# Weight loads between the adaLN loads of the first block, and a new order of loads and row ends in the last phase

## The chip, the cores and the metric

The kernel runs on one core of a Trainium2 chip. The metric is the device time of one execution, in microseconds; before the change the median of three runs is 3001.27 us. The engines are TensorE (PE, with its weight loads as PEld), VectorE (DVE), ScalarE (ACT), GpSimd (POOL) and SyncE (SP). In this kernel SP only issues DMAs, and it issues all of them, in one order that is fixed when the kernel is built.

## The reference

The input x has 2048 rows of 1024 channels. It is RMS-normalised, modulated by shift and scale that come from a condition vector (adaLN), and projected to all inputs of two branches: a gated causal convolution with a layer norm, and an RWKV-7 time mixing. Both are projected, gated, added, projected out and added to x; a final RMSNorm closes it.

```
mod = einsum('bd,de->be', silu(c), ada_w) + ada_b
shift, scale, gate = split(mod, 3)
h = rmsnorm(x, norm_g) * (1 + scale) + shift
p = h @ w_in
c_val, c_gate, c_og, ts, r_og, g_conv, g_rwkv = split(p)
y_conv = conv_branch(...)                      # ends in: silu(layernorm(u)) * silu(c_og) @ w_conv_out
y_rwkv = rwkv7_branch(...)                     # ends in: (layernorm(o) + bonus) * silu(r_og) @ w_rwkv_out
m = sigmoid(g_conv) * y_conv + sigmoid(g_rwkv) * y_rwkv
x = x + gate * (m @ w_out)
out = rmsnorm(x, final_g)
```

## The kernel before

The rows are worked in four blocks of 512 (TB), the channels in eight tiles of 128 (KT, k). Every large product is taken in single precision as three products of rounded halves: both operands are split into hi and lo, and hi by hi, lo by hi and hi by lo are summed in PSUM (mm3k, L207 to L215). A tile of 128 output columns is 24 matmuls of 512 columns, or in the first phase 48 of 256. Its weights are 512 KB; in block 0 load_w (L179) loads them as w_st (L189), ACT casts hi (L192), POOL or DVE subtracts for lo (L194), and both halves are stored to DRAM (L199, L200), from where later blocks load them ready made. The buffers for weights (tag w) are seven.

**First phase, block 0 (hprep0, L386).** Sixteen loads of 512 KB (L236) bring the adaLN rows for shift and scale, and DVE sums each of them against silu(c) (L237). From these come, per k, one column of shift and scale (ACT, L914 and L915). For each k PE transposes and normalises x (ps_x, L408), ACT applies shift and scale (hf, L411), ACT casts h_hi (L371) and DVE subtracts h_lo (L372). Four "front" tiles of the input projection run along with h: LORA, K, R and V (ps_f), whose weights are loaded at k = 0, 2, 4 and 5. The weights of R and V have buffers of their own (w_f). After them come the fifth tile, the low-rank products of the first pair of heads (aux<-lw,wl, L484), the pair's norms (ACT's sq, L519), its scores and solve (aux<-uv,As, L623, is the first product behind the scores), and so on through 70 further tiles.

**Last phase (L1014 on).** For each block the two branches' outputs are projected: rproj (eight tiles ps_main, times a gate into mr, L1023), then cproj (eight tiles, added to mr and split to m_hi, m_lo). The out-projection makes four column blocks (cb) of 256 columns, each of 96 matmuls in two accumulators pout (L1121 to L1123); addx (L1129) adds x to them on DVE, in two row tiles a buffer. finish (L1133 to L1144) ends a tile of 128 rows: a sum of squares, rsqrt in ten small DVE operations, two products with final_g (fg, L1142) and two stores. For the next block, osplit (L982 on) loads three operands for each of eight columns (ot, bt, rt, five buffers of tag ld), POOL adds and multiplies (L992, L993), ACT casts and DVE subtracts (L970, L971); lnorm (L1045 on) loads eight y (L1051), sums them on POOL (L1054), subtracts the mean (L1059), squares and sums (L1063), and makes u_hi, u_lo for the next cproj. Some names are reused by tiles of other stages, so that osplit's columns appear as m_lo<-ot,m_hi in the profile.

The order of the instructions on each engine is decided by a scheduler at build time that plays the program through with costs and priorities; "issue_after(ins)" adds that what stands under it follows ins on that engine. In block 0 the weight loads of the front had that condition on the last adaLN load issued so far, but the next adaLN load had none on them. In the last phase, osplit and lnorm of the next block were written ahead of the loads of x, and the finish of a block ahead of the next rproj.

## Time and profile before

| what | before |
|---|---|
| median of 3 runs (lowest, highest) | 3001.27 us (3000.13, 3005.64) |
| profiled execution | 3002.41 us |
| its span, granted clock of the core | 3000.7 us, 0.975 |
| busy: PE, DVE, ACT, POOL | 2817.7, 2049.1, 942.6, 1250.8 us |
| DMA: share of 16 engines' span in the hardware queue | 68.4% |

A row of a timeline gives start, duration, engine, line, operation, out<-in, the form, the count of merged instructions and, in brackets, the idle time before it with what ended it. A row of waits gives what the engine waited for, the total, how often, and the longest.

### The profile page before, as it was taken

The numbers are of one execution on the slowest core, as the hardware profiler recorded it, in microseconds if no ns is written. First come the engines' busy times: TensorE is split into PE (matmuls) and PEld (weight loads), VectorE is DVE, ScalarE is ACT, GpSimd is POOL, SyncE is SP. The second block draws the span as 40 slices with busy tenths as digits, with TensorE's granted clock in tenths as the row PEclk, the third lists the DMA queues.
The fourth block names the chain that finished last, engine by engine and source line by source line (L and its number), as shares of the span: only waits on it lengthen the run. The fifth ranks groups of instructions, "written<-read, shape, count | busy, mean of one in ns | idle before, by whom it ended". The sixth has DMA issues, their size and how long they took to land.

```text
span 3000.7 us, 64775 instructions
## 1 busy us (share of the span) xinstructions
PE 2817.7 (94%) x25672; PEld 2645.0 (88%) x25672; DVE 2049.1 (68%) x3871; ACT 942.6 (31%) x1779; POOL 1250.8 (42%) x1786
## 2 busy tenths in 40 slices
PE   6899998999999999899999989999999998899998
PEld 6889898989989989898999989999989988687988
DVE  6587878777767676867776767777689534768433
ACT  5433434332323242323231414132333212333201
POOL 3465555525343425243434355526367014555000
PEclk9999999999999999999999999999999999999999
DMA  8666758664768579747475777656547678879674
GB/s 314 210 239 215 252 202 289 229 219 153 265 194 282 163 252 299 233 152 228 144 245 164 253 241 249 206 184 194 181 160 279 219 266 305 319 285 347 241 282 168
DMA packets 367697, 699.24 MB, mean 233 GB/s; under 512 B 135265, under 2 KB 154017, under 8 KB 367394
## 3 DMA queue, kind: packets, MB, share of 16 engines
q1 hardware_dynamic: 367394, 695.10, 68.4%
q8 instruction: 202, 3.31, 0.4%
q14 instruction: 101, 0.83, 0.1%
HBM read 506.14 MB, written 187.70 MB: 231 GB/s over the span
## 4 chain that ended last, share of the span: by engine, by line
PE 44%; DMA 17%; DVE 14%; POOL 12%; issue 5%; SPq 4%; ACT 3%; POOLq 0%; DVEq 0%; ACTq 0%
PE ps_main L215 32%; POOL TT L653 4%; POOL itmp L651 4%; DMA La<-dA 2%; DMA w_st<-w_ro_t 2%; DMA w_st<-w_in_t 2%; DVE acc L800 2%; PE pout L1121 1%; PE pout L1122 1%; PE pout L1123 1%; PE aux L553 1%; DMA w_gr<-grow_d 1%; PE xo L715 1%; DMA w_st<-w_co_t 1%; SPq L637 1%
## 5 line engine op out<-in xcount | busy, mean ns | idle before, releaser
L215 PE MATMUL ps_main<-h_hi,w_hi 128*128 128x256 f32 x4608 | 947.4, 284 | 13.4 <-ACT w_hi L192 6.4
L215 PE MATMUL ps_main<-h_hi,w_lo 128*128 128x256 f32 x4608 | 948.5, 285 | 9.3 <-POOL w_lo L194 5.1
L215 PE MATMUL ps_main<-h_lo,w_hi 128*128 128x256 f32 x4608 | 954.6, 285 | 0.0
L215 PEld LDWEIGHTS ps_main<-h_hi,w_hi 128*128 128x128 f32 x4608 | 718.2, 191 | 24.8 <-ACT w_hi L192 7.1
L215 PEld LDWEIGHTS ps_main<-h_hi,w_lo 128*128 128x128 f32 x4608 | 717.2, 191 | 17.5 <-POOL w_lo L194 6.5
L215 PEld LDWEIGHTS ps_main<-h_lo,w_hi 128*128 128x128 f32 x4608 | 719.2, 191 | 8.6 <-issue 0.5
L800 DVE SCALAR_TENSOR_TENSOR acc<-u,ck,acc 128x512 f32<-128x512 f32 x928 | 697.9, 752 | 20.7
L651 POOL TENSOR_TENSOR itmp<-La,TT 128x126 f32<-128x126 f32 (+22 forms) x496 | 182.0, 367 | 162.6 <-DMA La<-dA 127.4
L653 POOL TENSOR_TENSOR TT<-TT,itmp 128x126 f32<-128x126 f32 (+22 forms) x496 | 188.0, 379 | 36.7
L707 ACT ACTIVATE Se<-S,pe 128x128 f32<-128x128 f32 x256 | 88.9, 394 | 243.9 <-DVE S L725 243.5
L194 POOL TENSOR_TENSOR w_lo<-w_st,w_hi 128x1024 fp32r<-128x1024 f32 x47 | 114.6, 2438 | 117.2 <-ACT w_hi L192 107.2
L725 DVE TENSOR_TENSOR S<-xo,Se 64x128 f32<-64x128 f32 x256 | 73.4, 287 | 99.4 <-PE xo L721 96.9
L192 ACT CAST w_hi<-w_st 128x1024 fp32r<-128x1024 f32 x71 | 74.4, 1048 | 193.8 <-DMA w_st<-w_in_t 159.1
L717 DVE TENSOR_TENSOR uv<-xo,rn 64x256 f32<-64x256 f32 x128 | 53.8, 420 | 95.1 <-PE xo L715 93.8
L712 DVE TENSOR_TENSOR XO<-xo,XO 128x256 f32<-128x256 f32 x128 | 53.7, 420 | 82.5 <-PE xo L710 65.2
L588 POOL TENSOR_TENSOR BK<-BK,pe 128x1024 f32<-128x1024 f32 x32 | 62.5, 1953 | 106.9 <-PE aux L553 86.4
L710 PE MATMUL xo<-S,KR 128*128 128x128 f32 x512 | 82.9, 284 | 19.6 <-DVE S L725 19.6
L563 DVE TENSOR_TENSOR As<-aux,maskA 128x512 f32<-128x512 f32 x128 | 82.8, 684 | 23.2 <-PE aux L553 22.1
L553 PE MATMUL aux<-KR,BK 64*128 64x128 f32 x1024 | 90.5, 293 | 8.3 <-POOL KR L541 5.1
L721 PE MATMUL xo<-uv,tk 128*128 128x128 f32 x512 | 81.8, 282 | 15.6 <-DVE uv L717 15.6
L715 PE MATMUL xo<-XO,As 64*64 64x64 f32 x1024 | 90.7, 227 | 5.5 <-DVE XO L712 5.4
L715 PEld LDWEIGHTS xo<-XO,As 64*64 64x64 f32 x1024 | 71.0, 136 | 25.7 <-DVE XO L712 6.7
(303 smaller groups left out, 5246.7 us busy)
## 6 DMA issues: line engine op xcount, KB each, us to landing
w_hi<-kh_in SPq DMA_DIRECT2D x219, 512.0 KB, 5.4
w_lo<-kl_in SPq DMA_DIRECT2D x219, 512.0 KB, 4.3
w_st<-w_in_t SPq DMA_DIRECT2D x73, 512.0 KB, 4.7
kh_in<-w_hi SPq DMA_DIRECT2D x71, 512.0 KB, 2.9
kl_in<-w_lo SPq DMA_DIRECT2D x71, 512.0 KB, 3.8
w_hi<-kh_ro SPq DMA_DIRECT2D x32, 512.0 KB, 6.3
w_lo<-kl_ro SPq DMA_DIRECT2D x32, 512.0 KB, 5.8
w_hi<-kh_co SPq DMA_DIRECT2D x32, 512.0 KB, 4.9
```

Of the source, the lines that this page charges most:

```text
L192: nc.scalar.copy(hi, st)
L194: lo_eng.tensor_tensor(out=lo, in0=st, in1=hi.bitcast(F32), op=ALU.subtract)
L215: nc.tensor.matmul(ps[:, qs], ww[:, k, :], aa[k][:, qs], start=(k == 0 and t == 0 and q == 0), stop=(k == KT - 1 and t == 2 and q == ms - ...
L553: return nc.tensor.matmul(pA[hh][:, c // 2, es], BK[hs, cc, es], KR[hs, cc, es], start=(c == 0), stop=(c == 3), skip_group_check=True)
L563: nc.vector.tensor_tensor(out=Asb[:, hh, c4 * 4:c4 * 4 + 4, :].rearrange("p (a e) n -> p a (e n)", e=2), in0=pA[hh], in1=flat(maskA).unsqu ...
L651: nc.gpsimd.tensor_tensor(out=tmp[:, :ni, :nt], in0=La[:, j:j + 1, j + 1:].broadcast_to([P, ni, nt]), in1=TT[:, :ni, j:j + 1].broadcast_to ...
L653: nc.gpsimd.tensor_tensor(out=TT[:, :ni, j + 1:], in0=TT[:, :ni, j + 1:], in1=tmp[:, :ni, :nt], op=ALU.add)
L707: nc.scalar.mul(Se[:, q, :], Sg[:, q, :], R[q]["pe"][:, c:c + 1])
L710: nc.tensor.matmul(xo[:, q, :], R[q]["KR"][:, cc, es], Sg[:, q, :], start=(q == 0), stop=(q == 1), skip_group_check=True)
L715: nc.tensor.matmul(xo[pr_, q, hs], As[q][pr_, hh, c, kcol(e)], XO[pr_, c, q, hs], start=(q == 0 and hh == 0), stop=(q == 1 and hh == 1), s ...
L721: last = nc.tensor.matmul(xo[:, 2 + q, :], R[q]["tk"][:, c, :], uv[:, c, q, :], start=False, stop=(q == 1), skip_group_check=True)
L800: nc.vector.scalar_tensor_tensor(out=acc if i + 1 < HALO else yj, in0=u[:, i:i + TB], scalar=ck[:, j, i:i + 1], in1=acc, op0=ALU.mult, op1 ...
```

## The change

It has three parts. In hprep0 each adaLN load behind the first follows the last weight load that was issued, so that the front's weights come between the adaLN loads; the stores and the small weights of the first pair follow the last adaLN load (front_ld). In the last phase, block 0 loads x first, and fg, osplit(1) and lnorm(1) issue their loads behind it. And finish of blocks 0 to 2 no longer stands ahead of the next rproj: two row tiles are finished behind its mr of n = 2, two behind n = 4.

```diff
     def load_w(name, n, hl=None, held=None):
...
-        nc.sync.dma_start(st, wsrc[name][n])
+        ada_ld[0] = nc.sync.dma_start(st, wsrc[name][n]).ins
...
         for k in range(KT):
-            next(ada_steps)
+            if k:
+                with tc.issue_after(ada_ld[0]):
+                    next(ada_steps)
+            else:
+                next(ada_steps)
...
+        front_ld.append(ada_ld[0])
         with tc.issue_after(ada_ld[0]):
             for store in held:
                 store()
...
-            with tc.issue_after(ada_ld[0]):
+            with tc.issue_after(front_ld[0]):
                 nc.sync.dma_start(wf, w2a2[pr])
...
-    def rproj(b, ohl, mr):
+    def rproj(b, ohl, mr, between=None):
...
-                nc.vector.scalar_tensor_tensor(out=mr[n], in0=th, scalar=1.0, in1=ppr, op0=ALU.add, op1=ALU.mult)
+                made = nc.vector.scalar_tensor_tensor(out=mr[n], in0=th, scalar=1.0, in1=ppr, op0=ALU.add, op1=ALU.mult)
+            if between and n in (2, 4):
+                with tc.issue_after(made.ins):
+                    for tt in (n - 2, n - 1):
+                        between(tt)
...
-    nc.sync.dma_start(fg, final_g.unsqueeze(0).broadcast_to([P, D]))
...
+    def xload(b):
...
+        return xts, ld.ins
+
+    for b in range(NB):
+        if b:
+            mhi, mlo = okt(b, MOFF)
+            cproj(b, uhl, (mhi, mlo))
+        if b == 0:
+            xts, ld = xload(0)
+            with tc.issue_after(ld):
+                nc.sync.dma_start(fg, final_g.unsqueeze(0).broadcast_to([P, D]))
+                ohl = osplit(1)
+                uhl = lnorm(1)
+        elif b + 1 < NB:
+            ohl = osplit(b + 1)
+            uhl = lnorm(b + 1)
+        if b:
+            xts, _ = xload(b)
...
         if b + 1 < NB:
-            for tt in range(NTT):
-                finish(tt)
-        if b + 1 < NB:
             mr = mnew()
-            rproj(b + 1, ohl, mr)
+            rproj(b + 1, ohl, mr, finish)
```

What it moves, at three places. SP's queue in the front, before: ada_st are the adaLN loads, w_st the weights (LORA, K, then R and V together, then the fifth tile), kh and kl the stores, ck and wf small operands.

```order
L236 DMA ada_st<-ada_t 128x1024 x5
L189 DMA w_st<-w_in_t 128x1024
L236 DMA ada_st<-ada_t 128x1024 x6
L199 DMA kh_in_830<-w_hi 128x1024
L200 DMA kl_in_831<-w_lo 128x1024
L434 DMA ck<-convk 128x248
L477 DMA wf<-w2a 128x256
L199 DMA kh_in_834<-w_hi 128x1024
L189 DMA w_st<-w_in_t 128x1024 x2
L200 DMA kl_in_835<-w_lo 128x1024
L189 DMA w_st<-w_in_t 128x1024
```

And with the change, from the same place on:

```order
L236 DMA ada_st<-ada_t 128x1024
L191 DMA w_st<-w_in_t 128x1024
L236 DMA ada_st<-ada_t 128x1024 x4
L191 DMA w_st<-w_in_t 128x1024
L236 DMA ada_st<-ada_t 128x1024 x2
L191 DMA w_st<-w_in_t 128x1024
L236 DMA ada_st<-ada_t 128x1024 x4
L201 DMA kh_in_830<-w_hi 128x1024
L202 DMA kl_in_831<-w_lo 128x1024
L201 DMA kh_in_834<-w_hi 128x1024
L202 DMA kl_in_835<-w_lo 128x1024
```

K's weights move four adaLN loads forward, those of R and V from behind the sixteenth to behind the tenth and the twelfth; the last four adaLN loads now follow V.

SP's queue in the out-projection of block 0, with the change (before, its order there is fg, then the eight y with the loads of osplit's fifth and sixth column between them, two ct, four xt, and only then the next w_lo and w_hi of the o projection; the loads of osplit's first four columns stand further ahead, among the weights of cproj). xt is x for rows 256 to 511; those for the first 256 rows stand earlier in both.

```order
L188 DMA w_lo<-kl_o_1_18069 128x1024
L187 DMA w_hi<-kh_o_0_19938 128x1024
L1108 DMA xt_31631<-x_in 128x512
L1108 DMA xt_31633<-x_in 128x512
L1108 DMA xt_31635<-x_in 128x512
L1108 DMA xt_31637<-x_in 128x512
L1120 DMA fg<-final_g 128x1024
L990 DMA ot<-o_d_0_75 128x512
L990 DMA bt<-bv_d_0_107 128x512
L990 DMA rt<-ro_d_0_139 128x512
L990 DMA ot<-o_d_1_76 128x512
L990 DMA bt<-bv_d_1_108 128x512
```

x stands ahead of y, and all columns of osplit(1), from the first on, stand behind x and fg; the eight y follow these rows, and behind the y the other weights of the o projection.

DVE at the start of rproj(1), before: rs is the rsqrt of the row ends, xt<-xt,rs,fg their products, and mr<-rth,ps_main what empties the accumulator of a tile of rproj (mr_32452 the first tile's).

```order
L133 SCALAR_TENSOR_TENSOR rs_t<-rs_t,vs 128x1 x2
L134 SCALAR_TENSOR_TENSOR rs_32379<-rs_t,rs_32379 128x1
L1136 TENSOR_REDUCE vs<-sq_31903 128x1
L134 SCALAR_TENSOR_TENSOR rs_32398<-rs_t,rs_32398 128x1
L1136 TENSOR_REDUCE vs<-sq_31903 128x1
L1142 SCALAR_TENSOR_TENSOR xt_31887<-xt_31887,rs_32379,fg 128x512
L1142 SCALAR_TENSOR_TENSOR xt_31889<-xt_31889,rs_32379,fg 128x512
L1142 SCALAR_TENSOR_TENSOR xt_31891<-xt_31891,rs_32398,fg 128x512
L1142 SCALAR_TENSOR_TENSOR xt_31893<-xt_31893,rs_32398,fg 128x512
L1137 TENSOR_SCALAR vs<-vs 128x1 x2
L971 TENSOR_TENSOR o_lo_33020<-ot,o_hi_33021 128x512
```

With the change (mr_32376 is the first tile's, mr_32378 the third's):

```order
L1084 TENSOR_SCALAR dg<-ident,rv 128x128 x4
L976 TENSOR_TENSOR m_lo_31654<-ot,m_hi_31646 128x512
L976 TENSOR_TENSOR m_lo_31655<-ot,m_hi_31647 128x512
L1028 SCALAR_TENSOR_TENSOR mr_32376<-rth,ps_main 128x512
L1028 SCALAR_TENSOR_TENSOR mr_32377<-rth,ps_main 128x512
L227 SCALAR_TENSOR_TENSOR y_31737<-th,y_31737 128x512
L1097 TENSOR_TENSOR y_31737<-y_31737,ct 128x512
L227 SCALAR_TENSOR_TENSOR y_31739<-th,y_31739 128x512
L227 SCALAR_TENSOR_TENSOR y_31742<-th,y_31742 128x512
L1097 TENSOR_TENSOR y_31739<-y_31739,ct 128x512
L976 TENSOR_TENSOR u_lo<-y_31737,u_hi 128x512
L1028 SCALAR_TENSOR_TENSOR mr_32378<-rth,ps_main 128x512
```

Before, the first mr stands three rows behind the last one quoted, after the ends of rows 0 and 1; now it follows osplit's last column, and the products of the first two row tiles stand between the fourth and the fifth mr.

11 lines of the change are left out of this document (2 added, 9 removed).

## The prediction

> **What bounds the kernel now.** I read the page first (busy times), then busy time in stretches to find where TensorE is not full, then PE's waits in those stretches, and last the timelines of the engines named there.
>
> ```profile
> PE 2817.7 (94%) x25672; PEld 2645.0 (88%) x25672; DVE 2049.1 (68%) x3871; ACT 942.6 (31%) x1779; POOL 1250.8 (42%) x1786
> ```
>
> PE is busy for 2817.7 of 3000.7 us, so a gain has to come out of the 183 us in which it stands still, or out of a clock below full. The change touches two places where that happens, the first 65 us and the stretch from 2500 to 2680. The columns are the stretch, its length, busy PE, PEld, DVE, ACT and POOL with counts, the granted clock, the DMA share and GB/s:
>
> ```profile
> 20.00:40.00 20.00, 18.06 (x127) 16.97 (x126) 20.00 (x31) 13.49 (x27) 2.74 (x2) 1.00 1.03 411
> 40.00:60.00 20.00, 14.56 (x96) 13.48 (x96) 7.52 (x13) 10.63 (x17) 8.61 (x5) 0.83 0.62 220
> 2500.00:2600.00 100.00, 81.90 (x528) 74.55 (x527) 65.28 (x138) 40.79 (x83) 56.37 (x43) 0.90 0.85 303
> 2600.00:2640.00 40.00, 35.85 (x149) 28.35 (x148) 16.75 (x22) 4.90 (x8) 22.16 (x15) 0.96 1.04 411
> 2640.00:2680.00 40.00, 39.89 (x206) 33.40 (x205) 25.68 (x43) 9.19 (x15) 16.62 (x12) 1.00 0.80 285
> ```
>
> At 20 to 40 us DVE has no gap and the DMAs are full; at 40 to 60 PE idles. From 2500 to 2600 PE idles 18 us, and from 2600 to 2640 the DMAs are full. What PE waits for in the first 125 us, and then from 2480 to the end (total, times, longest):
>
> ```profile
> PE aux L523 <- ACT sq L519: 5.9, 1, 5.9
> PE ps_f L215 <- ACT w_f L192: 4.5, 2, 3.6
> ```
>
> ```profile
> PE ps_main L215 <- DVE mr L1023: 13.1, 4, 9.3
> PE pout L1121 <- DVE xt L1129: 8.8, 2, 8.6
> ```
>
> **Part 1, the front.** PE's, ACT's and SP's rows show what is late; x2 and the like count merged instructions:
>
> ```profile
> 25.76 0.78 PE L215 MATMUL ps_f<-h_hi,w_hi 128*128 128x256 f32 x2
> ...
> 29.29 1.05 PE L408 MATMUL ps_x<-dg,x 128*128 128x128 f32 x8
> ...
> 48.20 0.79 PE L215 MATMUL ps_f<-h_hi,w_f 128*128 128x256 f32 x2 [3.61 <-ACT w_f L192]
> ...
> 62.84 0.39 PE L484 MATMUL aux<-lw,wl 128*128 128x512 f32 x1
> ...
> 122.43 1.15 PE L623 MATMUL aux<-uv,As 64*64 64x64 f32 x32
> ```
>
> ```profile
> 47.10 1.04 ACT L192 CAST w_f<-w_st 128x1024 fp32r<-128x1024 f32 x1
> ...
> 49.20 1.03 ACT L192 CAST w_f<-w_st 128x1024 fp32r<-128x1024 f32 x1
> ```
>
> ```profile
> 32.18 1.58 SPq L189 DMA_DIRECT2D w_st<-w_in_t  x2
> ```
>
> The last two front tiles, R and V (96 matmuls), start at 48.20 and end at 62.84, because their weights are issued at 32.18, behind all sixteen adaLN loads, and cast at 47.10 and 49.20. The change puts these loads behind the tenth and the twelfth adaLN load, and the casts go ahead of the last columns of h, so R and V run while h is made. Two bounds then hold. PE has 192 front matmuls from 25.76 on, at 6.00 / 54 = 0.111 us each, and four more ps_x groups of 1.05:
>
> ```profile
> 56.00:62.00 6.00, 6.00 (x54) 1.00 1.00 364
> ```
>
> That gives 25.76 + 21.3 + 4.2 = 51.3. The other bound is the last column of h, which DVE ends:
>
> ```profile
> 28.64 1.21 DVE L237 SCALAR_TENSOR_TENSOR ada_st<-ada_st,srow 128x1024 f32<-128x1024 f32 x1
> ...
> 30.39 3.40 DVE L237 SCALAR_TENSOR_TENSOR ada_st<-ada_st,srow 128x1024 f32<-128x1024 f32 x1
> ...
> 42.65 0.69 DVE L372 TENSOR_TENSOR h_lo<-hf,h_hi 128x512 fp32r<-128x512 f32 x1 [1.31 <-ACT h_hi L371]
> ```
>
> ```profile
> 30.07 2.64 POOL L194 TENSOR_TENSOR w_lo<-w_st,w_hi 128x1024 fp32r<-128x1024 f32 x1 [9.98 <-ACT w_hi L192]
> ```
>
> An adaLN accumulation takes 1.21 us, but 3.40 beside POOL's subtraction for w_lo. Two more such subtractions now fall among the accumulations, so h ends at 43.3 + 2 x 2.2 = 47.7, and its last column feeds 24 matmuls, 2.7 us, less what PE has finished of the others: 49 to 50.4. PE's own 51.3 is later. With small gaps (it idled 1.9 of the 20 us from 20 to 40) the front ends at 53.5 and not at 62.84: 9 us, 11.5 at most. If the loads come so late that half of the old wait stays, 5.
>
> The Trainium skill says of this in GPSIMD Engine Reference, in its table of the engine, that GpSimd shares its SBUF interfaces with VectorE, with contention for DVE instructions that have two SBUF inputs; it speaks against the change, and the 3.40 beside 1.21 agrees with it. If by that rule a DVE instruction lost the whole 2.64 us of each subtraction, h would end at 48.6, still behind PE's 51.3.
>
> How much of it reaches the first use of the attention scores, at 122.43? Next come the fifth tile and pair 0's chain; both orders do the same PE work up to there. PE now runs the fifth tile straight behind the front and may wait up to 2.6 us for its w_lo (one subtraction of POOL). ACT's square, for which PE waited 5.9 us, has the two late casts no longer beside it, worth 2 x 1.04 and at most the whole 5.9. So from 0 (the chain of weights and stores behind the front, which now follows later adaLN loads in SP's queue, ends as late as ever) to 9 + 5.9 = 15. I take 9 + 2.1 = **11 us**. The scheduler has also shifted rows across the rest of block 0, with no wait removed or added that I can name: 0, with 6 us either way, which is one of the waits above, as bound.
>
> **Part 2, the last phase, block 0.** Two stalls and what follows each:
>
> ```profile
> 2527.72 0.58 PE L1121 MATMUL pout<-w_hi,o_hi 128*128 128x256 f32 x1 [8.65 <-DVE xt L1129]
> ...
> 2583.99 0.79 PE L215 MATMUL ps_main<-m_hi,w_hi 128*128 128x512 f32 x1 [9.27 <-DVE mr L1023]
> ...
> 2731.65 0.50 PE L215 MATMUL ps_main<-o_hi,w_hi 128*128 128x512 f32 x1 [2.72 <-DVE mr L1023]
> ```
>
> ```profile
> 2527.70:2533.00 5.30, 5.28 (x26) 5.04 (x26) 0.42 (x1) 1.29 (x5) 4.11 (x4) 0.58 1.02 412
> 2584.00:2590.50 6.50, 6.50 (x16) 5.10 (x17) 6.50 (x27) 5.00 (x8) 1.04 (x1) 0.52 0.99 358
> 2590.50:2597.00 6.50, 6.50 (x31) 5.34 (x30) 6.50 (x10) 4.33 (x7) 0.82 (x1) 1.00 1.04 385
> ```
>
> After the 8.65 us wait the clock is 0.58 for 5.3 us, 2.2 lost; after the 9.27 one it is 0.52 for 6.5, 3.1 lost. Together the two stalls hold 23.2 us. Their causes:
>
> ```profile
> 2471.28 0.32 SPq L985 DMA_DIRECT2D ot<-o_d  x1
> ...
> 2510.10 4.39 SPq L1051 DMA_DIRECT2D y<-y_d  x5
> ...
> 2520.72 2.20 SPq L1105 DMA_DIRECT2D xt<-x_in  x4
> ```
>
> ```profile
> 2525.84 1.09 DVE L971 TENSOR_TENSOR m_lo<-ot,m_hi 128x512 fp32r<-128x512 f32 x1 [11.15 <-ACT m_hi L970]
> ...
> 2532.58 0.69 DVE L971 TENSOR_TENSOR m_lo<-ot,m_hi 128x512 fp32r<-128x512 f32 x1 [4.91 <-ACT m_hi L970]
> ...
> 2543.69 1.11 DVE L971 TENSOR_TENSOR m_lo<-ot,m_hi 128x512 fp32r<-128x512 f32 x1 [3.09 <-ACT m_hi L970]
> ...
> 2574.78 6.77 DVE L1142 SCALAR_TENSOR_TENSOR xt<-xt,rs,fg 128x512 f32<-128x512 f32 x4
> ...
> 2583.26 0.67 DVE L1023 SCALAR_TENSOR_TENSOR mr<-rth,ps_main 128x512 f32<-128x512 f32 x1
> ```
>
> x is issued behind eight y's; ahead of them it comes some 9 us earlier, so the first wait falls to 0 to 2. The mr that frees PE's buffer stands behind the finish of rows 0 and 1 on DVE; the change takes that chain away from it. But the price is in the same place: osplit(1), whose first four columns were loaded from 2471 on and done by 2515, now has all eight behind x and fg, and rproj(1) needs them all for its first tile. The late four of before came (2543.69 - 2525.84) / 3 = 6.0 us apart. From a first column at 2521, the eighth is at 2521 + 7 x 6.0 = 2563, so most of the first stall comes back as a wait of rproj's first tile. That tile ends near 2564, the next 5 us later (24 matmuls at 6.5 / 31), the pieces of lnorm between them take 3, and the third tile starts at 2572. Before it started at 2583.99, and 3.1 more were lost to the clock: 15 us.
>
> Not all of it stays. The twelve early loads, 3.1 MB, now fall behind 2500, 7.6 us of DMA at 411 GB/s. Of 100 us at share 0.85, 15 were free, so 7.4 remain; at 2600 to 2640 none were, and at 2640 to 2680 8 are. The DMAs therefore allow 7 to 15 us. DVE also has the finishes to do a few tiles later, between the next mr's, each beside POOL work:
>
> ```profile
> 2564.28 1.30 POOL L992 TENSOR_TENSOR ot<-ot,bt 128x512 f32<-128x512 f32 x1 [3.09 <-DVE rs L129]
> ...
> 2568.47 10.86 POOL L1086 TENSOR_TENSOR y<-y,rl 128x512 f32<-128x512 f32 x8
> ```
>
> Once more 6.77 us for two rows' products can stand ahead of an mr, where a tile gives DVE 5 us and a second buffer covers it. I take **9 us**, nearer the DMAs' bound than the 15, with -2 to 15. The removed weight of y in the queue costs lnorm nothing that shows: its output is wanted only after eight rproj tiles, about 40 us later.
>
> **Part 3, blocks 1 and 2.** The same move of finish takes away the 2.72 us before block 2's third tile; no slow clock followed that one. I take **2 us**, from -2 (the finish falls ahead of another mr) to 4. In block 2 no such wait stands in the 13.1 above, so 0. The final block's finish is unchanged.
>
> **Sum.** 11 + 9 + 2 = 22 us. The profiled execution took 3002.41 us; 3002.4 - 22 = 2980.4. The median of the runs, 3001.27, lies 1.1 lower, so I predict **2979 us**, by itself 2969 to 2989.
>
> **Rivals.** (A) The osplit columns take over the whole of block 0's gain in the last phase: at 7.5 us apart, the eighth comes at 2573.5 and the third tile starts at 2583. For it: 6.7 us between 2525.84 and the next, and eight columns' POOL work (2 x 1.30 each, 20.8 us) beside fourteen sums of y's statistics. Against it: 6.0 is the mean with the same neighbours. The time is 3001.3 - 11 - 2 = 2988. Chance 0.14. (B) The front's gain is hidden: pair 0's chain starts from weights that still come one after another, and 122.43 stays. For it: PE idles in this stretch whatever the front does. Against it: the chain's PE work stands behind the front's in PE's order, so an earlier front lets it start earlier. 3001.3 - 11 = 2990, 0.11. (C) Both are hidden, or the reordering of block 0 takes them back: about 3000, 0.10. (D) Slower: SP issues in order, and a column that waits for one of its five load buffers holds the out-projection's weights behind it, so that both PE's tiles and the next column slip. It decides from 8.1 us a column, where 2521 + 7 x 8.1 + 9 passes 2587. At 11 us a column the third tile starts at 2607, 20 later than before, with another slow clock of 3; less 13 from the other parts, 3011. Against it: the old queue mixed the same loads with weights at 6.0. Chance 0.08. My forecast has 0.57.
>
> **How the numbers follow.** About 0.2%, 6 us, is what a measurement of this kernel can tell from no change. Faster: the forecast, A and B, 0.82, less 0.01 for A and B falling short, 0.81. Same: C and that, 0.11. Slower: 0.08. The range of 8 in 10 reaches over A and B to the edge of C and, below, to both parts at their best (3001 - 15 - 15 - 4 = 2967, and a few us of luck in block 0): 2964 to 2999.
>
> **What would show it.** Right: front matmuls end at 52 to 56, the w_f waits are gone, DVE has two more long accumulations; aux<-uv,As comes at 108 to 115; no pout wait on xt above 2 us, a new wait of rproj's first tile on m_lo, no long wait on mr for the third. Wrong: 122 again; columns more than 7 us apart; a wait on weights of the o projection; another slow clock near 2590.

## The result and the profile after

The changed kernel takes 2992.84 us, median of 18 runs (2987.89 to 3002.53), against 3001.61 of the kernel before beside it (2996.95 to 3012.06, 18 runs): a ratio of 0.9967 [0.9956, 0.9978], about 9.9 us less. Ratios, here and below, are against the kernel before on the same chip, with a 95% interval in brackets, and leave out three slow executions of 3669 us and more. The forecast was 2979, 22 us less; the direction is right, the size is not. The profiled execution took 2994.08 us (span 2992.4, granted clock 0.977), 8.3 less than the one before.

The page's busy times after the change:

```profile
PE 2818.5 (94%) x25672; PEld 2644.7 (88%) x25672; DVE 2057.4 (69%) x3871; ACT 941.4 (31%) x1779; POOL 1260.4 (42%) x1786
```

PE does the same work in the same time, so the 8.3 us came out of its idle time. The same stretches as before the change:

```profile
20.00:40.00 20.00, 16.40 (x129) 15.32 (x129) 18.84 (x24) 11.43 (x22) 8.22 (x3) 1.00 1.03 414
40.00:60.00 20.00, 17.90 (x151) 17.43 (x150) 12.28 (x23) 11.22 (x20) 3.48 (x3) 1.00 0.66 254
2500.00:2600.00 100.00, 88.44 (x555) 77.96 (x554) 58.94 (x108) 36.51 (x76) 68.13 (x47) 0.97 0.92 327
2600.00:2640.00 40.00, 34.32 (x143) 26.00 (x142) 26.53 (x52) 9.73 (x17) 21.05 (x15) 1.00 1.04 404
2640.00:2680.00 40.00, 40.00 (x258) 36.15 (x257) 36.63 (x47) 17.13 (x29) 31.40 (x20) 1.00 0.87 316
```

From 40 to 60 us PE has 151 matmuls where it had 96, and its clock is not lowered any more. From 2500 to 2600 it is busy 88.4 us, was 81.9, and POOL 68.1, was 56.4. Of these 11.8 us, 5.1 are osplit's adds and multiplies (27.5 before, 32.7 now: eleven columns where ten were, and each operation longer); most of the rest is lnorm's work. PE's waits of the changed kernel, in the first 125 us and then from 2480 on:

```profile
PE late L359 <- DVE xt L356: 4.8, 1, 4.8
PE ps_main L217 <- DVE carry L457: 4.4, 2, 3.8
PE ps_main L217 <- ACT w_hi L194: 2.2, 1, 2.2
```

```profile
PE ps_main L217 <- DVE mr L1028: 10.7, 4, 4.9
PE ps_main L217 <- DVE cth L1014: 3.6, 2, 2.4
PE pout L1142 <- DMA w_lo<-kl_o: 3.5, 1, 3.5
```

The waits on w_f, on ACT's square and of pout on xt are gone; new ones have come at other places, and mr is still what PE waits for most in the last phase. In time the front looks like this: the last front matmuls, and the first product behind the scores.

```profile
53.33 0.39 PE L217 MATMUL ps_f<-h_hi,w_f 128*128 128x256 f32 x2
...
118.21 2.08 PE L628 MATMUL aux<-uv,As 64*64 64x64 f32 x64
```

The front ends at 53.7 (62.84 before), the scores are used at 118.21 (122.43 before).

**Where the time went.** One execution of a program differs from the next by several us, so the traces are compared by stages. The last phase starts at PE's first out-projection matmul of block 0 (first row of pout). In the four traces with the old first phase (the kernel before, and the experiments e2, e3 and e4, which leave the first phase as it was) it starts at 2503.9 to 2509.5, mean 2507.3; in the sixteen with the new one at 2488.7 to 2509.3, mean 2496.2: 11.1 us earlier. From the out-projection of block 2 on, the rest of the last phase, 188 us, differs by less than 1 us between the kernel before and the change. For the stretch between, the matmul rows of PE's timeline were added up by their columns, and the table gives the time, from its first pout, at which a share of them is done, up to the first pout of block 2. So kernels are compared at equal PE work. "Old order" is the mean of four traces with the last phase of before (the kernel before and three of the front alone), "change" that of four with the changed one (the change three times, and its last phase alone); the others are one trace each. Counted matmul by matmul, by their starts, single marks lie up to 1.1 us from these (2.1 in e12) and the differences between the two means up to 0.5.

```
                               20%   26%   30%   40%   50%   75%   80%   all
old order of the last phase   66.6  94.1 105.0 138.9 166.4 238.6 253.3 306.0
change                        63.0  82.5 101.6 132.4 162.6 232.5 253.5 307.6
e3  x ahead, ends as before   61.9  93.8 105.5 132.3 161.7 230.8 252.1 304.3
e4  ends moved, x as before   66.5  86.2 107.0 143.0 170.2 239.8 253.3 306.5
e7  no row ends               85.9 111.1 123.6 151.3 181.0 250.9 264.5 317.2
e8  bt, rt loaded once        65.9  82.6 101.1 147.7 173.8 245.5 259.2 313.3
e9  ends moved in block 0     64.4  83.4 101.6 136.3 164.8 235.5 254.7 311.9
e10 ends behind rproj         64.5  83.4  96.0 127.7 173.6 242.1 255.3 309.1
e11 y behind weights          64.4  87.9 101.0 139.0 166.6 243.7 258.1 312.4
e12 osplit free               65.0  81.0 102.2 142.0 168.5 243.6 258.7 310.5
e15 row ends bare             63.1  81.9  95.1 130.5 161.0 230.9 244.7 297.8
e16 osplit without POOL       64.1  79.9  93.4 130.5 159.2 228.8 242.2 295.3
e17 joint ends, change        63.9  82.6  98.0 134.1 166.6 237.1 256.9 311.4
e18 joint ends, old order     65.9  94.9 105.3 133.9 162.5 239.3 253.8 306.6
```

At 26%, in the fifth tile of rproj(1), the change is 11.6 us ahead. At 30% it has lost 8.2 of that, at 75% it is 6.1 ahead, and at 80% it is level: one twentieth of the work takes 21.0 us where the old order takes 14.7. At the end it is 1.6 behind. The four traces of the change lie within 4.1 us of each other at every mark (305.8 to 308.7 at the end), those of the old order within 4.9.

So the whole measured gain is the first phase's, 11.1 - 1.6 = 9.5, against 9.9 by the ratio; the two parts in the last phase, forecast at 11 us, bring nothing.

The two places where it is lost, in PE's timeline of the change: the sixth tile of rproj(1) and, after a shorter wait in cproj(1), the sixth of rproj(2).

```profile
2587.36 0.50 PE L217 MATMUL ps_main<-m_hi,w_hi 128*128 128x512 f32 x1 [4.13 <-DVE mr L1028]
...
2637.26 0.50 PE L217 MATMUL ps_main<-u_hi,w_hi 128*128 128x512 f32 x1 [2.41 <-DVE cth L1014]
...
2739.42 0.80 PE L217 MATMUL ps_main<-o_hi,w_hi 128*128 128x512 f32 x1 [4.86 <-DVE mr L1028]
```

A view of stretches around the last of these, of the change:

```profile
2730.00:2740.00 10.00, 5.14 (x22) 3.94 (x21) 10.00 (x20) 0.62 (x1) 5.71 (x5) 0.92 0.38 109
2740.00:2745.00 5.00, 5.00 (x13) 3.92 (x12) 5.00 (x29) 0.00 (x0) 0.00 (x0) 0.50 1.04 378
```

And around the third tile of rproj(2) of the kernel before, whose wait was 2.72:

```profile
2726.50:2731.70 5.20, 2.48 (x10) 1.38 (x9) 5.20 (x16) 0.62 (x1) 1.96 (x2) 1.00 0.79 282
2731.70:2740.00 8.30, 7.69 (x33) 5.99 (x34) 8.30 (x25) 1.39 (x3) 1.86 (x2) 1.00 1.00 317
```

The wait that was to go has moved three tiles on and grown from 2.72 to 4.86 us, and the clock behind it is 0.50 for the 5 us of the row, 2.5 us lost in it, where before it stayed at 1.00. The Trainium skill, in TensorE: Matmul & The Clock Gate, section "Why this matters for your kernels", warns of idle gaps above some 3 us; a wait of 2.72 without and waits of 4.86, 8.65 and 9.27 with a lowered clock agree with that. But shorter waits were followed by a lower clock too, 2.76 us in e3 (0.66 from 2745 to 2755) and 2.12 us in e1 (0.66 from 2699.5 to 2704.5), so these traces do not show 3 us as a limit.

DVE's timeline shows what stands ahead of that mr (x2: for two row tiles):

```profile
2725.03 0.68 DVE L1028 SCALAR_TENSOR_TENSOR mr<-rth,ps_main 128x512 f32<-128x512 f32 x1
2725.63 0.21 DVE L1156 TENSOR_REDUCE vs<-sq 128x1 f32<-128x4 f32 x2
...
2726.18 1.35 DVE L132 TENSOR_TENSOR rs_t<-rs 128x1 f32<-128x1 f32 x2
2727.45 0.27 DVE L133 SCALAR_TENSOR_TENSOR rs_t<-rs_t,vs 128x1 f32<-128x1 f32 x2
2727.64 1.32 DVE L134 SCALAR_TENSOR_TENSOR rs<-rs_t,rs 128x1 f32<-128x1 f32 x2
2728.93 1.34 DVE L132 TENSOR_TENSOR rs_t<-rs 128x1 f32<-128x1 f32 x2
...
2736.03 2.74 DVE L1162 SCALAR_TENSOR_TENSOR xt<-xt,rs,fg 128x512 f32<-128x512 f32 x4
2738.69 1.28 DVE L1028 SCALAR_TENSOR_TENSOR mr<-rth,ps_main 128x512 f32<-128x512 f32 x2
```

The finish of two rows follows the mr of n = 2, as written, and takes from 2725.63 to 2738.7, 13 us, of which the small operations of the rsqrt take 10.4 (one m_lo of 1.79 stands among them). A tile of PE's is 5.4 us at full clock here, and two buffers cover two of them. The mr of the fourth and fifth tile come after it, both in the row at 2738.69, and so the sixth tile, which needs one of their two buffers, starts at 2739.42.

### The profile page after: what moved, and what is told of

Its sections match the earlier page's. It is cut to its first block, busy times and chain, and to the rows that moved or that the text cites. A ratio compares the mean times of both kernels' runs of the same rounds, so it can differ in the third digit from the quotient of the medians.

```text
span 2992.4 us, 64781 instructions
## 1 busy us (share of the span) xinstructions
PE 2818.5 (94%) x25672; PEld 2644.7 (88%) x25672; DVE 2057.4 (69%) x3871; ACT 941.4 (31%) x1779; POOL 1260.4 (42%) x1786
## 4 chain that ended last, share of the span: by engine, by line
PE 45%; DMA 13%; DVE 13%; POOL 8%; issue 4%; SPq 3%; ACT 2%; DVEq 0%; POOLq 0%; ACTq 0%
PE ps_main L217 32%; DVE acc L805 3%; POOL TT L658 3%; POOL itmp L656 2%; DMA w_st<-w_ro_t 2%; PE pout L1142 2%; PE pout L1143 2%; PE pout L1141 2%; DMA w_gr<-grow_d 2%; PE xo L720 1%; PE aux L558 1%; DMA xt<-x_in 1%; DMA La<-dA 1%; PE xo L715 1%; PE xo L726 1%
## 5 line engine op out<-in xcount | busy, mean ns | idle before, releaser
L217 PE MATMUL ps_main<-h_hi,w_hi 128*128 128x256 f32 x4608 | 951.0, 285 | 19.1 <-ACT w_hi L194 9.1
L217 PE MATMUL ps_main<-h_hi,w_lo 128*128 128x256 f32 x4608 | 951.4, 285 | 14.7 <-POOL w_lo L196 9.8
L715 PE MATMUL xo<-S,KR 128*128 128x128 f32 x512 | 83.0, 285 | 19.1 <-DVE S L730 19.1
L758 POOL TENSOR_TENSOR XO<-XO,gst 128x1024 f32<-128x1024 f32 x16 | 30.5, 1907 | 166.0 <-DVE gst L757 166.0
L817 ACT ACTIVATE th<-ps_main 128x512 f32<-128x512 f32 x64 | 38.2, 597 | 182.7 <-PE ps_main L217 166.7
```

What stands on the lines that cost most here:

```text
L217: nc.tensor.matmul(ps[:, qs], ww[:, k, :], aa[k][:, qs], start=(k == 0 and t == 0 and q == 0), stop=(k == KT - 1 and t == 2 and q == ms - ...
L715: nc.tensor.matmul(xo[:, q, :], R[q]["KR"][:, cc, es], Sg[:, q, :], start=(q == 0), stop=(q == 1), skip_group_check=True)
```

## The experiments

**The parts alone.** The first part alone has the hunks of load_w, ada_cols, hprep0 and the pair's weights (wf); the others alone have those of rproj and of the last phase.

```diff
 e1: only
+                with tc.issue_after(ada_ld[0]):
+                    next(ada_steps)
...
 e2: only
+    def xload(b):
...
+            rproj(b + 1, ohl, mr, finish)
```

> Only the first part of the change (weight loads between the adaLN loads); the last phase stays as before. Its order in the first phase is the one of the whole change. Theory A (the prediction's): the front's 9 to 11 us stay to the end, ratio about 0.9963. Theory B (the front's gain is taken back in block 0, where later waits take its place, and what is left comes from reordered rows): ratio 0.998 to 1.000, and the third pair's solve starts no earlier than before. Theory C: all of the measured 10 us come from here (0.9967) and the last phase gives nothing.

> Only the parts in the last phase (x ahead of y, osplit(1) and lnorm(1) behind x, finish between the next tiles); the first phase is exactly in its old order. Theory A (the prediction's): 11 us faster, ratio 0.9963. Theory B (the last phase gains in block 0 and gives a part back in block 1): 3 to 6 us faster, 0.998 to 0.999. Theory C: nothing, 1.000.

e1: 0.9942 [0.9919, 0.9964]. e2: 0.9985 [0.9968, 1.0003]. The front alone brings all of the gain. That it brings more than the whole change is not borne out by two further runs of it (e5 and e13), each with the whole change beside it (e6 and e14).

> Once more only the first part, now on the same chip as the whole change (next run). The first study gave 0.9942 (0.9919 to 0.9964) for it and 0.9967 (0.9956 to 0.9978) for the whole change. If the last phase's parts are worth nothing: both the same within 0.2%, near 0.996. If they cost something in this company: this one 3 us or more ahead of the whole change. If they gain as predicted: the whole change 9 to 11 us ahead.

> The whole change beside the run above: 0.9967 as before if that measurement holds; level with the front alone if the last phase's parts give nothing, 0.3% ahead of it if the prediction's part 2 and 3 are there and were hidden by chance.

> Only the first part, a third time, beside the whole change on one chip. If the last phase's parts are worth nothing, both are level within 3 us; if they cost, as the traces of the last phase hint (498.4 us from the end of the first phase in the front alone, 498 to 501 with the whole change), this one is 1 to 5 us ahead.

> The whole change beside the run above: ratio near 0.9967 again, and 0 to 5 us behind the front alone.

The front alone: 0.9955 [0.994, 0.997] and 0.9963 [0.9948, 0.9977]. The change: 0.9966 [0.9951, 0.998] beside the first of these and 0.9963 [0.9949, 0.9977] beside the second. They are level within what the runs can tell, with the front alone never behind.

**The last phase divided.** e3 has e2's order of loads and the finish where it was; e4 the moved finish and the old order of loads.

```diff
 e3, against e2
         if b + 1 < NB:
+            for tt in range(NTT):
+                finish(tt)
+        if b + 1 < NB:
             mr = mnew()
-            rproj(b + 1, ohl, mr, finish)
+            rproj(b + 1, ohl, mr)
 e4, against before
-            for tt in range(NTT):
-                finish(tt)
...
+            rproj(b + 1, ohl, mr, finish)
```

> Only x ahead of y with osplit(1), lnorm(1) and fg behind x; finish stays ahead of the next tiles as before; the first phase is in its old order. If the wait on x alone is worth what its row says and the columns of osplit take most of it back (the prediction's step), 0 to 4 us faster, ratio 0.9987 to 1.000, with a wait of about 9 us or more on mr still there. If the finish moves out of the way by itself, 8 us faster.

> Only the finish of blocks 0 to 2 between the next tiles; loads in the old order, and the first phase too. The prediction's step: the 9.27 us wait and its slow clock go in block 0 (12 us, of which the DMAs allow 7 to 12), and 2 us more in block 1: 9 to 14 us faster, ratio 0.9953 to 0.997. If block 1 loses by it (a wait of 4 to 5 us on mr in place of 2.7, and a slow clock behind it): 3 to 7 us faster, ratio 0.9977 to 0.999, with that wait in the trace of block 1.

0.9994 [0.998, 1.0008] and 0.9997 [0.9982, 1.0012]: neither does anything by itself. In the table each does its part and gives it back. e3 is 4.7 us ahead at 20% (the first stall is gone) and 7.8 at 75%; between 75 and 80% it takes 21.3 us (14.7 in the old order), with waits on pvar's qs (2.76) and w_lo and a clock of 0.66 for 10 us. e4 is 7.9 ahead at 26% (its third tile has no 9 us wait) and 4.1 behind at 40%. Its waits on mr, the longest 4.72, come at later tiles, and then PE waits 5.56 us on cproj's cth.

So the stalls are not removed by either order: in e4 DVE is late a few tiles on, in e3 PE waits in block 1 for POOL's sums of squares.

**Is it the DMAs?** The prediction bounded the block-0 part by DMA time. e8 loads bt and rt once for each block, 14 loads of 256 KB less, and so leaves out the right operands for seven of the eight columns. bt and rt get a buffer each, ot keeps four of the five.

```diff
-        t_ = ob.tile([P, TB], F32, name=name, tag="ld", bufs=5)
+        t_ = ob.tile([P, TB], F32, name=name, tag="ld", bufs=4)
...
+        bt, rt = [ob.tile([P, TB], F32, name=n_, tag="once" + n_, bufs=1) for n_ in ("bt", "rt")]
+        nc.sync.dma_start(bt, bv_dram[b][0])
+        nc.sync.dma_start(rt, ro_dram[b][0])
...
-            ot, bt, rt = ldt("ot", o_dram[b][j]), ldt("bt", bv_dram[b][j]), ldt("rt", ro_dram[b][j])
+            ot = ldt("ot", o_dram[b][j])
```

> The whole change, but osplit loads its second and third operand once a block and uses them for all eight columns: 14 loads, 3.7 MB or 9 us of DMA, less in each block; POOL's, DVE's and PE's work is the same (one load buffer fewer, so the two kept tiles have room). Theory DMA: 5 to 15 us ahead of the whole change. Theory DVE: 0 to 3 us ahead, and the waits on mr stay.

0.9991 [0.9979, 1.0003], slower than the change if anything, and 313.3 us in the table. At 411 GB/s these 14 loads, 3.7 MB, are 9 us; taking them away gains nothing. This alone does not clear the DMAs, because the order in SP's queue moved too: four ot now stand together ahead of the y and the weights, and PE waits 6.70 us on w_lo in the out-projection (3.52 in the change), 5.75 on mr and 4.97 on u_hi. Two experiments below, e15 and e16, keep every load and are 9.8 and 12.3 us shorter in the table; it is they that show that the amount of DMA does not set this stretch.

**Is it the row ends on DVE?** e7 leaves out finish for blocks 0 to 2 but for its stores. Its rows of these blocks are not normalised.

```diff
+                if b + 1 < NB:
+                    for half in range(2):
+                        nc.sync.dma_start(out[t0:t0 + P, half * 512:half * 512 + 512], xts[tt][half])
+                    return
```

> The whole change, but the finish of blocks 0 to 2 leaves out its DVE work (mean square, rsqrt, products with rs and fg): the rows are stored as they are. Stores, loads and PE's work stay. Theory DVE (the row ends are only moved to another mr, and DVE in rproj(1) and rproj(2) bounds PE there): 8 us or more ahead of the whole change, no wait on mr above 1 us. Theory DMA (full DMAs from 2580 to 2640 and 2740 to 2760 set the pace, and what PE gains before is waited for there): within 3 us of the whole change, with waits on weights or x in place of mr.

1.0008 [0.9997, 1.0019], 317.2 us: slower, and inconclusive. Without DVE work ahead of them the stores and the next x went to the front of SP's queue, osplit's loads slid behind, and rproj's first tiles waited for their input:

```profile
2579.80 1.22 PE L217 MATMUL ps_main<-m_hi,w_hi 128*128 128x512 f32 x2 [17.46 <-ACT m_hi L975]
```

e15 mends that: one DVE operation on four columns for each half row stays, so SP's queue keeps its order. Here too the rows of blocks 0 to 2 are not normalised.

```diff
+                        nc.vector.tensor_scalar(out=xts[tt][half][:, 0:4], in0=xts[tt][half][:, 0:4], scalar1=1.0,
+                                                scalar2=None, op0=ALU.mult)
```

> The whole change, but the finish of blocks 0 to 2 does only a product of four columns for each half row on DVE and stores: the mean square, the rsqrt and the products with rs and fg are left out, and the stores keep their place in SP's queue. Theory DVE (the row ends hold mr between the tiles): the waits of 4.1, 1.4 and 4.9 us on mr go, and the last phase is 8 to 15 us shorter than the change's. Theory of another bound (y's chain over POOL, ACT and DVE is wanted by cproj at the same time whatever rproj does): the waits move to u or cth in cproj, and it is within 4 us of the change.

0.9946 [0.9929, 0.9962] against 0.9963 of the change on the same chip; 297.8 us in the table, 9.8 less than the change. It takes 13.2 us from 26 to 30% (change 19.1) and 13.8 from 75 to 80% (change 21.0). The wait of 4.86 is gone; of PE's waits on mr this is left:

```profile
PE ps_main L217 <- DVE mr L1028: 2.0, 2, 1.7
```

**Or osplit's work on POOL?** e16 keeps osplit's loads and cuts POOL's add and multiply to 4 of 512 columns; the operand of rproj is then not the sum and product that it should be.

```diff
-            nc.gpsimd.tensor_tensor(out=ot, in0=ot, in1=bt, op=ALU.add)
-            EN[OE].tensor_tensor(out=ot, in0=ot, in1=rt, op=ALU.mult)
+            for t_ in (bt, rt):
+                nc.gpsimd.tensor_tensor(out=ot[:, 0:4], in0=ot[:, 0:4], in1=t_[:, 0:4], op=ALU.add)
```

> The whole change, but osplit's add and product on POOL are done for four columns only, not for 512, in every block: 16 POOL operations of 1.3 us less in each of blocks 1 to 3, the loads stay. Theory POOL (POOL's queue, and DVE's small operations at 1.3 us in place of 0.2 beside it, bound the stretch from 2500 to 2760): the last phase is 8 us or more shorter than the change's, and DVE's rsqrt operations are short. If POOL is not it: within 4 us.

0.99 [0.9887, 0.9913], 2971.86 us. In the table it gains 12.3 us on the change, 7.6 of them from 75 to 80%, though every row end is still there. Some 6 us of its lead in the median lie outside this stretch; what they are stays open. DVE's timeline at the same place shows why the row ends no longer hurt:

```profile
2718.28 0.22 DVE L1156 TENSOR_REDUCE vs<-sq 128x1 f32<-128x4 f32 x2
...
2718.84 0.23 DVE L132 TENSOR_TENSOR rs_t<-rs 128x1 f32<-128x1 f32 x2
...
2720.39 0.23 DVE L134 SCALAR_TENSOR_TENSOR rs<-rs_t,rs 128x1 f32<-128x1 f32 x2
2720.59 2.74 DVE L1162 SCALAR_TENSOR_TENSOR xt<-xt,rs,fg 128x512 f32<-128x512 f32 x4
2723.25 0.67 DVE L1028 SCALAR_TENSOR_TENSOR mr<-rth,ps_main 128x512 f32<-128x512 f32 x1
```

The small operations take 2.3 us instead of 10.4, and the whole finish 5. So e15 shows what the row ends take, and these rows that they take it because POOL works beside them. e4 agrees: with all of osplit's work in place, the same operations for the first two row tiles of block 1 run from 2745.76 to 2747.88 there, 2.1 us, while POOL stands still from 2744.5 to 2756.1. But e16 does not price osplit's work alone. In the change lnorm's y<-y,pmean stand ahead of these row ends on DVE, and five of the seven POOL operations beside them are lnorm's sums of squares; only two are osplit's. In e16 the scheduler has put y<-y,pmean behind the finish, and the sums start at 2725.9, after it. How much of the 12.3 us is the shorter work and how much this order stays open.

**Other places and orders.** If the place of the row ends or of y were at fault, another would gain. e9 moves the ends in block 0 only; e10 puts all four behind the last mr of rproj; e11 is e9 with y's loads behind the last but two pieces of the out-projection's weights; e12 is e11 with osplit's loads not held behind x.

```diff
 e9, against the change
+        if b and b + 1 < NB:
+            for tt in range(NTT):
+                finish(tt)
...
-            rproj(b + 1, ohl, mr, finish)
+            rproj(b + 1, ohl, mr, None if b else finish)
 e10, against the change
-            if between and n in (2, 4):
+            if between and n == KT - 1:
...
-                    for tt in (n - 2, n - 1):
+                    for tt in range(NTT):
 e11, against e9
-                uhl = lnorm(1)
...
+                if b == 0 and (cb, kh) == (2, 1):
+                    with tc.issue_after(lastw[0]):
+                        uhl = lnorm(1)
 e12, against e11
+            ohl = osplit(1)
             xts, ld = xload(0)
...
-                ohl = osplit(1)
```

> The whole change, but from block 1 on finish stands ahead of the next rproj as before; block 0 keeps it behind the third and fifth tile. In three traces of the change's last phase PE waits 4.86 to 4.87 us on mr in block 1, with a slow clock behind it, and DVE spends 10 us on the ten small rsqrt operations of two row tiles, each 1.3 us beside POOL's work in place of 0.2. If that is what block 1 costs: that wait is gone or at most 2.7 us, as before, and the last phase 3 to 6 us shorter than the change's. If the wait comes back in another place in block 1: within 2 us.

> The whole change, but all four row tiles of blocks 0 to 2 are finished behind the last mr of the next rproj. If the row ends between the tiles are what PE waits for (waits on mr of 4.1, 1.4 and 4.9 us, each with the slow clock): those are gone and the last phase is 5 to 10 us shorter than the change's, unless x of the next block, whose buffers come free later, is now waited for in the next out-projection. If DVE's other work (y, u_lo) holds mr: the waits in block 0 stay, and only block 1 gains 3 to 5 us.

> As the first of these runs (row ends between the tiles in block 0 alone), and lnorm(1) issues its loads behind the third column block's weights of the o projection. The wait of 3.5 to 4.5 us on w_lo in the out-projection of block 0 stands behind eight y in SP's queue in all traces with x ahead: it should go, with 2 us of slow clock. 4 to 6 us shorter in the out-projection, if osplit's columns, which then come alone on POOL, are there in time; 0 if rproj's first tile then waits for them instead, or lnorm is late for cproj.

> As the run before, and osplit(1) is no longer held behind x: its first columns load among cproj's weights, as before the change. The prediction said that osplit behind x gives most of the first stall back: then this gains 3 to 8 us on the run before, at rproj's first tile. If the columns are no bound (in the change's trace rproj's first tile waits under 1 us for them): 0, since the 7.6 us of DMA only move.

0.9972 [0.9958, 0.9986], 0.9967 [0.9954, 0.998], 0.997 [0.9957, 0.9983] and 0.9967 [0.9953, 0.9981]: all four level with the change. e10 is the plainest. It is the fastest of all orders at 40% (127.7) and takes 13.2 us from 75 to 80%, but pays in cproj. The ends run there from 2605 to 2622, and ahead of a later cth stand five rows of lnorm's y on DVE, 1.64 to 1.77 us each beside POOL's y<-y,rl, where the same take 0.68 elsewhere:

```profile
2663.92 0.80 PE L217 MATMUL ps_main<-u_hi,w_hi 128*128 128x512 f32 x1 [8.39 <-DVE cth L1014]
```

Its step from 40 to 50% is 45.9 us (change 30.2). In e11 the wait of 3.52 on w_lo is gone, with 1.88 on a w_hi of the o projection left, but it takes 23.5 us from 20 to 26%, where the change takes 19.5. e12's third tile does not wait, but its sixth waits 7.98, longer than in the change:

```profile
2586.81 0.80 PE L218 MATMUL ps_main<-m_hi,w_hi 128*128 128x512 f32 x1 [7.98 <-DVE mr L1029]
```

**Fewer small operations.** If each of the small operations cost, one chain for four row tiles instead of four chains would help. e17 does that to the change, e18 to e1.

```diff
+            def ends(tt):
+                if tt == 0:
+                    rs4[0] = v4 = f2.tile([P, 3, NTT], F32, name="v4", tag="v4", bufs=1)
+                    nc.vector.tensor_reduce(out=v4[:, 0, :], in_=sq4, axis=AX.X, op=ALU.add)
...
+                    rsqrt(v4[:, 1, :], v4[:, 0, :], None, nc.vector, v4[:, 2, :])
...
-            rproj(b + 1, ohl, mr, finish)
+            rproj(b + 1, ohl, mr, ends)
```

> The whole change, with the mean square and rsqrt of all four row tiles of a block taken in one chain of twelve operations on four columns in place of four chains on one column; the products and stores stay where they are. Result unchanged. If DVE's row ends beside POOL's work are what PE waits for in rproj, as the runs without them show (last phase 9 to 10 us shorter), this takes a third to a half of that: 3 to 5 us ahead of the whole change, ratio near 0.995, and the wait of 4.9 us on mr in block 1 falls below 2. If only the large products count: within 1 us of the change.

> Only the first part of the change, finish ahead of the next rproj as before, but with the same single chain for four row tiles. The waits of 7.5 us on mr in rproj(1) and of 2 to 3 in rproj(2) shrink by what the small operations take there: 2 to 5 us ahead of the front alone, ratio near 0.995.

0.9994 [0.998, 1.0007] and 1.0005 [0.9991, 1.0019]: no gain, and by the ratios about 9 and 15 us more than the kernels that they start from. The chain, now one for each block where two pairs were, takes as long as one pair did. DVE's timeline of e17:

```profile
2742.46 0.15 DVE L1170 TENSOR_REDUCE v<-sq 128x4 f32<-128x16 f32 x1
...
2744.41 0.16 DVE L132 TENSOR_TENSOR v<-v 128x4 f32<-128x4 f32 x1
2744.61 1.15 DVE L133 SCALAR_TENSOR_TENSOR v<-v 128x4 f32<-128x4 f32 x1
2745.79 0.16 DVE L134 SCALAR_TENSOR_TENSOR v<-v 128x4 f32<-128x4 f32 x1
2745.98 1.15 DVE L132 TENSOR_TENSOR v<-v 128x4 f32<-128x4 f32 x1
...
2752.92 2.74 DVE L1177 SCALAR_TENSOR_TENSOR xt<-xt,v,fg 128x512 f32<-128x512 f32 x4
```

And POOL's beside it:

```profile
2743.06 5.43 POOL L1072 TENSOR_TENSOR qs<-qs,sq 128x512 f32<-128x512 f32 x4
```

From 2742.46 to 2752.92 it is again 10.5 us. What costs is the steps that are held, not the width of the chain. Of the 9 and 15 us the table shows 3.8 and 0.6; the first phase, which they leave alone, ended at 2509.3 and 2498.2, later than the mean of 2496.2 (the traced execution of e17 is the slowest of its twelve). The rest is open, and shows that a few tenths of a per cent between two programs can't be put down to one edit by the ratio alone.

No kernel that computes the reference was clearly faster than the change; the front alone is level with it or better, with fewer edits.

## Why the prediction was right and wrong

**Part 1, 11 us: the sum held, by a partly different way.** The front came out as worked out: 53.5 was predicted for its end, 53.7 measured; 47.7 for the last h_lo, and it ends at 48.6 (that this is also the 48.6 of the prediction's other estimate is chance). The way there differs. The sign "two more long accumulations" came only by half: the kernel before has two of them (3.18 and 3.40 us), the change three (3.18, 3.38 and 3.42). The other subtraction made an h_lo long, 1.81 where it takes 0.68 alone, and DVE waited 0.97 and 0.77 us for ACT's h_hi:

```profile
34.76 1.81 DVE L372 TENSOR_TENSOR h_lo<-hf,h_hi 128x512 fp32r<-128x512 f32 x1 [0.97 <-ACT h_hi L371]
36.50 3.42 DVE L237 SCALAR_TENSOR_TENSOR ada_st<-ada_st,srow 128x1024 f32<-128x1024 f32 x1
...
47.89 0.69 DVE L372 TENSOR_TENSOR h_lo<-hf,h_hi 128x512 fp32r<-128x512 f32 x1 [1.32 <-ACT h_hi L371]
```

What failed is the step to the scores: "9 + 2.1" was to arrive at 108 to 115, and they come at 118.21, 4.2 earlier than before. PE waits there for things I had not named: xt 4.8, the carry 3.8, w_hi 2.2. The rest of the 11.1 us comes later, out of the reordered rows for which I took "0, with 6 us either way". At equal PE work the traces with the new first phase are some 5 to 8 us ahead from 500 us on, and 12 behind 1480. Two waits of the kernel before, 2.57 us on KR at 1406.84 and 4.09 on vv at 1417.25, account for about 5 of that step; the change has one of 1.22 there, on BK at 1415.82.

So the 11 is right partly by luck: 4 of it was foreseen, and 7 was in the term that I had booked at nothing.

**Part 2, 9 us: right up to the third tile, and then gone. This is the step that failed**, with the choice "nearer the DMAs' bound than the 15". The first wait went as foretold (8.65 to 0.64), and the third tile was to start at 2572 on the time scale of before, 68.1 us after that kernel's first pout at 2503.9. It starts at 2566.61, 68.0 after 2498.6. At 26% of the work the change is 11.6 ahead. The predicted wait of rproj's first tile on m_lo, which was to eat up most of the first stall, did not come (the longest on an m_lo is 0.58); one of 3.52 on the o projection's weights came instead:

```profile
2526.89 0.58 PE L1142 MATMUL pout<-w_lo,o_hi 128*128 128x256 f32 x1 [3.52 <-DMA w_lo<-kl_o]
...
2566.61 0.50 PE L217 MATMUL ps_main<-m_hi,w_hi 128*128 128x512 f32 x1 [0.31 <-DVE mr L1028]
```

But I stopped there. I wrote that two rows' products "can stand ahead of an mr" and that "a second buffer covers it", with 6.77 us as their price. It did not cover it: the mr of the fourth tile is 10.2 us behind that of the third.

```profile
2576.41 0.68 DVE L1028 SCALAR_TENSOR_TENSOR mr<-rth,ps_main 128x512 f32<-128x512 f32 x1
...
2578.12 1.78 DVE L976 TENSOR_TENSOR u_lo<-y,u_hi 128x512 fp32r<-128x512 f32 x1
...
2579.95 1.65 DVE L227 SCALAR_TENSOR_TENSOR y<-th,y 128x512 f32<-128x512 f32 x1
...
2583.59 1.30 DVE L133 SCALAR_TENSOR_TENSOR rs_t<-rs_t,vs 128x1 f32<-128x1 f32 x2
...
2585.42 1.29 DVE L134 SCALAR_TENSOR_TENSOR rs<-rs_t,rs 128x1 f32<-128x1 f32 x2
2586.63 0.67 DVE L1028 SCALAR_TENSOR_TENSOR mr<-rth,ps_main 128x512 f32<-128x512 f32 x1
```

Between the two stand seven rows of lnorm's y and u_lo, 7.2 us together, three of them 1.06 to 1.78 long where the others take 0.68, and 3.4 us of the row ends' small operations. So the price was not that of the products: it was lnorm's work and the first steps of the rsqrt, part of both slowed beside POOL. mr is late at the sixth tile (4.13), cth at cproj (2.41), and at half of the work 3.8 of the 11.6 are left. Without the row ends (e15) the step from 26 to 30% is 5.9 us shorter, so they are most of the 8.2 lost there. I also bounded the part by DMA time, 7 to 15 us, and put the moved columns' adds and multiplies on POOL in no term of the sum (rival A names 20.8 us of them). e15 and e16 keep the loads and are 9.8 and 12.3 us shorter, so it was not the amount of DMA that took the gain. e16, without most of osplit's work on POOL and with another order on DVE, gains 3.4 more at half of the work and loses nothing in block 1.

**Part 3, 2 us: the wrong sign.** "The same move of finish takes away the 2.72 us before block 2's third tile": it did, and three tiles later stands 4.86 with a slow clock. From 75 to 80% this is 6.3 us, and it takes all that was left of part 2. The bound of -2 was too narrow for the same reason: the chain was priced with the row of the products, not with the ten small operations beside POOL. But the move by itself does no harm there: in e4, which has the moved ends without x ahead, that step is 13.5. In e3 and e9, with x ahead and the old place of the ends in block 1, it is 21.3 and 19.2, hardly better than 21.0; with x ahead and bare ends (e15) it is 13.8. So in these traces, one each but for the change, it takes both, x ahead and the row ends, at either place. I had priced the parts as if they added up. How x ahead does it stays open. It moves osplit's columns: the view of the tile ot on POOL shows osplit's adds (count, minimum, median and maximum ns, first and last start) from 2640 to block 2's first pout, in the change

```profile
L997 POOL TENSOR_TENSOR ot<-ot,bt x10: 1281/1566/1742, 2640.7 to 2731.6; 128x512 f32<-128x512 f32 x10
```

and before:

```profile
L992 POOL TENSOR_TENSOR ot<-ot,bt x6: 1267/1328/1777, 2647.0 to 2750.8; 128x512 f32<-128x512 f32 x6
```

Ten columns, the last two of osplit(2) and all of osplit(3), against six of osplit(3). e3 has ten as well, e4 seven. But the more of them lie ahead of rproj(2); beside the 10.4 us of the row ends stand two operations of osplit's and five of lnorm's sums of squares. So that the columns are what holds the row ends is not shown.

**The rivals.** A's time, 2988, is nearer than mine, but its mechanism did not happen: the columns did not hold rproj's third tile. B (front hidden) came in part, since only 4.2 of the front's 9.1 us reach the scores; but the 11.1 us at the start of the last phase speak against B and C as forecast. D's hold of weights behind a column is there in small, 3.52 us. A rival that I should have had is that the waits on DVE's mr come back a few tiles later at equal sum: its time is 3001.3 - 11 = 2990.

What stays open: how x ahead and the row ends work together in block 1, why e17 and e18 lose more than the last phase shows, and which part of block 0's reordering gives the 5 to 8 us between 500 and 1400, where two executions of one program differ by as much.

## What to carry to other kernels

A wait that is removed on one engine is worth its length only if the engine that it waited for has time to spare in the tiles that follow: follow that engine's queue to the end of the stage and add up its work, not only the first row that comes free. Parts of a change that touch the same stage are tried alone and together before their gains are added. Work that is moved into a stage has a price on each engine that touches it, and where two engines slow each other that price has to be taken from rows where both are busy. When single executions differ by as much as the effect, compare traces stage by stage at equal work, with several executions of each order.

## What the runs showed of the hardware

In e17 some of the small DVE operations take 0.15 or 0.16 us, others, beside POOL, 1.15 to 1.25; a row of two of them, 0.23 in e16, takes 1.25 to 1.35 in the change. The rows show where the time goes. In the change POOL's four sums run from 2726.22, 1.35 us each (5.40 / 4), so they end at about 2727.57, 2728.92, 2730.27 and 2731.6:

```profile
2726.22 5.40 POOL L1072 TENSOR_TENSOR qs<-qs,sq 128x512 f32<-128x512 f32 x4
```

DVE's rows that begin at 2726.18, 2727.64 and 2728.93 end at 2727.53, 2728.96 and 2730.27. Each stands beside a running POOL operation and ends with it, within 0.05 us; the row between the first two slips through in 0.27. Of the nine steps from the first L132 on, six rows are long in the change (1.25 to 1.35) and five in e17. So what a chain of dependent steps costs is the POOL work that runs beside it, whatever its width: 10.4 us with two chains of one column, 10.5 with one of four, 2.3 with POOL still. The sums of squares and scalings ahead of it (0.21, 0.22) were not held in the change, though POOL worked there too. The Trainium skill states the mechanism, in SBUF — State Buffer, section "SBUF: two separate sides": the shared port pair "is an exclusive lock, not a bandwidth split", and a DVE operation with two SBUF inputs waits while GpSimd has it. The ends of these rows agree with it. One row of e17 has one input and is held all the same, a TENSOR_SCALAR on 128x4 that takes 1.22 us at 2743.16 and ends with POOL's first sum (2743.06 + 1.36); on 128x1, in the change, the same step takes 0.15 beside POOL. No run here shows what makes the difference.
